# A transformer layer's up-projection: sums moved from GpSimd to VectorE, one block of work spaced wider, one norm written to other tiles

## The chip, the cores and the metric

The kernel runs on one core of a Trainium2 chip. The metric is the device time of one execution in microseconds (us). The kernel before took 2619.06 us (median of three runs, 2615.29 to 2621.99). A profile is one further execution, recorded by the hardware profiler.

The engines are named as the profile names them: PE is TensorE (matrix multiplications), DVE is VectorE, ACT is ScalarE, POOL is GpSimd, SP is SyncE, which here only starts DMA transfers. Each takes its instructions strictly in the order in which they were written for it. An instruction that has to wait holds everything behind it on the same engine.

## The reference

One layer of a diffusion transformer works on 2048 tokens of width 1024, with retention and grouped attention side by side, an output projection, and a feed-forward part of width 4096, all in float32. What matters here is the end of the layer:

```
x  = x + g1 * (concat([ret, att]) @ w_out)
h2 = rmsnorm(x, norm2_g) * (1 + sc2) + sh2
x  = x + g2 * (square(relu(h2 @ w_ff1)) @ w_ff2)
return rmsnorm(x, final_norm_g)
```

`h2 @ w_ff1` is the up-projection, the product with `w_ff2` the down-projection. The part `g2 * (... @ w_ff2)` is computed with g2 multiplied into the columns of `w_ff2`.

## The kernel before

**Numbers.** A float32 matrix is used as two fp16 matrices, a high part (ScalarE rounds) and a low part (VectorE subtracts the high part from the source). Each product of two such matrices takes three multiplications, high by high, high by low and low by high. The two 2x2 block matrices of each product in the feed-forward part are multiplied in the Strassen-Winograd way: seven products P1 to P7 instead of eight, of sums and differences of the blocks. These sums must be made for all three inputs: for `w_ff1` (w1), for h2 (h) and for `w_ff2` (w2).

**Up-projection.** `w_ff1` is cut into 16 blocks of 256 columns, the tokens into two halves. There are 24 items (`ITEMS`): first eight blocks with the first half, then the other eight with both halves, then the first eight with the second half. An item has seven products per half, in the order P1, P2, P6, P5, P7, P3, P4; P6, P7 and P4 accumulate onto P1's PSUM bank, P3 onto P5's. Between these, ScalarE copies the bank (`tap`, L2103) or VectorE adds it to an earlier copy (`add`, L2107), so a product that goes on with a bank waits until the copy or addition before it has read that bank. After an addition ScalarE applies relu (L2108, L2129) and the square (L2112), and SP stores the result (L2135). The first four products are made at the end of the stage before; the other 220 (`JOBS`) are numbered 0 to 219: items with one half are products 0 to 51, items with both halves 52 to 163, the last eight items 164 to 219. One product is twelve multiplications (L2092, L2093, L2094) into 512 columns.

**What each item needs of w1.** `fetch_w1` loads a block two items ahead (L2048, SP, into a ring of four tiles, two per item); `sum_w1` makes four sums of 128x512 float32 (L2060, GpSimd); `hi_w1` (L2065, ScalarE) and `lo_w1` (L2071, VectorE) make the seven high and low parts.

**What runs beside the products.** `h_forms`, four times from product 5 on, ten products apart, forms the second token half of h: four sums (in `seven`, L2154, GpSimd), seven high parts (L2179, ScalarE) and seven low parts (L2184, VectorE and GpSimd in turn). `w2_forms`, sixteen times from product 53 on, forms a block of w2: loads (L2144), a product with g2 of 128x1024 for each of two tiles (`gated`, L2150, GpSimd), the four sums of `seven` (L2154), seven high parts (L2208), seven low parts (L2212), and stores to DRAM (L2216). For products P2 and P4 of w2 (in the last of four rounds only P2) a second level of the scheme is formed: differences of 128x256 (`minus`, L2231, GpSimd), one for each of the first two blocks of a round and three for each of the other two, 56 in all. The tiles of the sums in `seven` come from a ring whose first three buffers have the tag "hu".

**The order** is written out by hand: `on(k, phase, ...)` puts a piece of work at product k, and within a product the phases follow as "begin", "pe", "sum", "hi", "lo", "relu", "out", "square", "late", "dma". So a sum at product k stands on its engine ahead of the low part at product k and of the addition at the end of product k.

**The last row before it.** `output_tile` makes the 16 rows (128 tokens each) of `x + g1 * ...`. The last one, t = 0, ends just as the up-projection begins: the row is stored (`store_x`, L1862), its root mean square is found (L1866, L1566, L1567), the row is multiplied by it in its own tile (`norm`, L1872, GpSimd), and then, in the `rest` steps at product 2 and after, TensorE transposes it (L1877), VectorE scales (L1882), GpSimd shifts (L1887) and SP stores it as h (L1890). The sums of w1 of items 0 and 1 stand on GpSimd around this norm.

**The down-projection** starts after product 219. Its first loads (`fetch_u`, `fetch_w2`) stand on SP from product 210 and 166 on; its sums (L2375, L2391) are on GpSimd.

Of the kernel before, what the change touches and what calls it, by code (L numbers as in the profile page):

```python
# [11 lines left out]
F32 = mybir.dt.float32  # L12
# [5 lines left out]
ALU = mybir.AluOpType  # L18
# [4 lines left out]
P = 128  # L23
# [33 lines left out]
def layer_kernel(ctx: ExitStack, tc: tile.TileContext, a: dict, out: bass.AP):  # L57
    nc = tc.nc
# [5 lines left out]
    ident = const.tile([P, P], F32, name="ident")  # L64
# [215 lines left out]
    with ExitStack() as st, tc.manual_schedule():  # L280
        xp = st.enter_context(tc.tile_pool(name="xp", bufs=4, reuse_waits="tile"))
# [4 lines left out]
        op = st.enter_context(tc.tile_pool(name="op", bufs=2, reuse_waits="tile"))  # L286
# [920 lines left out]
        units, first = [], {}  # L1207
# [10 lines left out]
        for (g, col), w in weights.items():  # L1218
            s = first[g, col]
# [13 lines left out]
        for n, (col, s) in enumerate(((C_RK, 5), (C_AKV, 6), (C_AQ, 12), (C_RQ, 16), (C_RV, 18), (C_RG, 26))):  # L1233
            w = weights[0, col]
            for j in range(w.n):
                at = s + (j if col != C_RV else j > 0)
                to = 1536 + 4 * n if col != C_RG else 1560
# [5 lines left out]
        for n, tile_of in enumerate(GROUPS[1]):  # L1243
            b = first[0, C_RV] + 3 + n + n // 6
            rows, x = Rows([tile_of], 1), {}
# [36 lines left out]
        s = first[1, C_RG]  # L1282
# [210 lines left out]
        for s, (g, col, m) in enumerate(units):  # L1493
            if s < 6:
                continue
            ps = psO.tile([P, 512], F32, name="pso", tag="pso")
# [8 lines left out]
        s = len(units)  # L1505
# [9 lines left out]
    def pool(stack, name, bufs=1, **kw):  # L1515
        return stack.enter_context(tc.tile_pool(name=name, bufs=bufs, reuse_waits="tile", **kw))

    qp = pool(attn, "qp", 2)
    op = pool(attn, "op2", 2)
# [5 lines left out]
    xp = pool(side, "wx", 2, side="right")  # L1525
# [14 lines left out]
    def bank(i, shape=(P, 4, P)):  # L1540
        return psX.tile(list(shape), F32, name=f"bank{i}", tag=f"bank{i}")
# [3 lines left out]
    def on(k, phase, fn, *args):  # L1545
        events.setdefault((k, phase), []).append((fn, args))
# [12 lines left out]
    def settle(what):  # L1559
        while what not in settled:  # L1560
            link()
# [254 lines left out]
    def output_tile(t, k, last):  # L1816
        y = {}
# [51 lines left out]

        def norm():  # L1870
            settle(("f", t))
            nc.gpsimd.tensor_scalar(y["x"], y["x"], y["r"], 1.0, op0=ALU.mult, op1=ALU.mult)  # L1872

        def transpose_x(q):
            y["ps", q] = bank(q if t < 2 else 1)
            for i in range(4):
                nc.tensor.transpose(y["ps", q][:, i], y["x"][:, (4 * q + i) * P : (4 * q + i + 1) * P], ident)  # L1877

        def modulate(q):
            s = slice(4 * q, 4 * q + 4)  # L1880
# [157 lines left out]
    raw1, w1 = {}, {}  # L2038
# [17 lines left out]
    def sum_w1(n, i):  # L2056
        if n < len(ITEMS):
            to, x, y, op = SUMS1[i]
            s = raw1[n, to] = xp.tile([P, 4, P], F32, name="w1s", tag="w1s", bufs=W1S)
            nc.gpsimd.tensor_tensor(s, raw1[n, x], raw1[n, y], op=op)  # L2060

    def hi_w1(n, i):
        if n < len(ITEMS):
# [73 lines left out]
    def seven(b0, source, tiles, gate=False):  # L2137


        x = {}  # L2140

        def fetch(g):
            w = ff["b"].tile([P, 2, 512], F32, "b")
            nc.sync.dma_start(w.rearrange("p a b -> p (a b)"), source(g))  # L2144
            x.update(zip(tiles(g), (w[:, 0], w[:, 1])))
            x["raw", g] = w.rearrange("p a b -> p (a b)")

        def gated(g):
            w = x["raw", g]
            nc.gpsimd.tensor_tensor(w, w, ff["g2"], op=ALU.mult)  # L2150

        def add(to, p, q, at=None):
            x[to] = x[at] if at else ff["bs"].tile([P, 512], F32, "bs")
            nc.gpsimd.tensor_tensor(x[to], x[p], x[q], op=ALU.subtract)  # L2154

        for g in range(2):
            on(b0 - (8 if gate else 5) + g, "dma", fetch, g)
            if gate:
                on(b0 - 2 + g, "sum", gated, g)
        sums = [("t1", "b12", "b11"), ("t2", "b22", "t1"), ("t3", "b22", "b12", "b12"), ("t4", "b21", "t2", "t1")]  # L2160
        for at, s in zip((0, 1, 2, 4), sums):
            on(b0 + at, "sum", add, *s)
        return x
# [28 lines left out]
    def w2_forms(b0, b):  # L2192
        rd, slot = PLACE[b]
        odd, s = slot // 2, slot % 2
        x = seven(
            b0,
            lambda f: a["w_ff2"][0, b * FB + f * P : b * FB + (f + 1) * P, :],
            lambda f: (f"b{f + 1}1", f"b{f + 1}2"),
            True,
        )  # L2200

        def split(at, dst, parts):
            f = {}

            def hi():
                f[0] = ff["w2f"].tile([P, 2, 512], F16, "w2f")
                for hi, _, src in parts(f[0]):
                    nc.scalar.activation(hi, src, AF.Copy)  # L2208

            def lo():  # L2210
                for hi, lo, src in parts(f[0]):
                    nc.vector.tensor_tensor(lo, src, hi, op=ALU.subtract)  # L2212

            def store():
                n = dst.shape[1] if len(dst.shape) == 3 else 1
                nc.sync.dma_start(dst, f[0] if n == 2 else f[0][:, 0])  # L2216

            on(at, "hi", hi)
            on(at + 1, "lo", lo)
            on(at + 3, "dma", store)  # L2220

        def pieces(f, *srcs):
            f = f.rearrange("p q (v n) -> p q v n", v=2)
            if len(srcs) == 1 and srcs[0].shape[-1] == 512:
                return [(f[:, :, 0], f[:, :, 1], srcs[0].rearrange("p (q n) -> p q n", q=2))]
            return [(f[:, q, 0], f[:, q, 1], src) for q, src in enumerate(srcs)]

        L, R = slice(0, 256), slice(256, 512)

        def minus(to, p, q):  # L2230
            nc.gpsimd.tensor_tensor(to(), p(), q(), op=ALU.subtract)  # L2231

        def deep(w, k):
            i = WORDS[w]
            to = wf_d[rd][i]

            def part(c):
                return lambda: x[w][:, c]

            def held(c):  # L2240
                return lambda: kept[i][:, c]

            def hold():
                nc.scalar.activation(kept[i][:, R], x[w][:, R], AF.Copy)

            def first():
                kept[i] = ff["k"].tile([P, 512], F32, name="w2k", tag=f"k{i}")
                minus(held(L), part(R), part(L))

            if not odd:  # L2250
                on(k, "sum", first)
                on(k + 2, "hi", hold)
                split(k + 2, to[:, 0:4:3, s], lambda f: pieces(f, x[w][:, L], kept[i][:, L]))
                return
            on(k, "sum", minus, held(L), part(R), held(L))
            on(k, "sum", minus, held(R), part(R), held(R))
            split(k + 2, to[:, 2:5:2, s], lambda f: pieces(f, kept[i]))
            split(k + 3, to[:, 1:6:4, s], lambda f: pieces(f, x[w]))
            on(k + 4, "sum", minus, held(L), part(L), held(L))
            split(k + 6, to[:, 6, s], lambda f: pieces(f, kept[i][:, L]))  # L2260

        for at, w in enumerate(WORDS):
            if WORDS[w] in DEEP[rd]:
                deep(w, b0 + (0 if w == "b21" else 5))
            else:
                split(
                    b0 + at,
                    wf_d[rd][WORDS[w]][:, slot],
                    lambda f, w=w: [(f[:, 0], f[:, 1], x[w])],
                )  # L2270
# [29 lines left out]
    def up_jobs():  # L2300

        first = {}
        for j, (n, i, hf) in enumerate(JOBS):
            first.setdefault((n, i), j)
            for k in range(4):
                on(j, "pe", up_part, n, i, hf, k)
            on(j, "out", up_out, j, n, i, hf)
        for n in range(len(ITEMS) - 1):
            for i in range(7):
                if (n, i) in first:  # L2310
                    at = first[n, i] + len(ITEMS[n][1]) - 1
                    at += 3 * (n == 1)
                    on(at, "hi", hi_w1, n + 1, i)
                    on(at + 1, "lo", lo_w1, n + 1, i)
            on(first.get((n, 0), 0), "dma", fetch_w1, n + 2)
            if n > 0:
                for i in range(2):
                    on(first[n - 1, 5 + i] + 2 * (n == 1), "sum", sum_w1, n + 1, i)
                    on(first[n, i] + 2 * (n == 1), "sum", sum_w1, n + 1, 2 + i)
        on(11, "dma", lambda: nc.sync.dma_start(ff["g2"], gate_d[1].partition_broadcast(P)))  # L2320
        on(20, "late", lambda: nc.scalar.activation(ff["g2"], ff["g2"], AF.Copy, scale=scw))
        for j in range(4):
            h_forms(5 + 10 * j, j)
        first1 = first[AHEAD, 0]
        for m, b in enumerate(PLACE):
            w2_forms(first1 + 1 + (8 * m if m < 14 else 11 * m - 32), b)
        for i in range(7):
            on(first[NB, 0] + 2 + 6 * i, "dma", fetch_w2, i)

# [319 lines left out]
```

## Time and profile before

| | |
|---|---|
| profiled execution | 2618.28 us |
| its span, first to last instruction | 2616.4 us |
| median of three runs | 2619.06 us |
| granted TensorE clock, mean | 0.996 |
| PE busy | 2577.8 us (99%) |
| DVE busy | 2133.8 us (82%) |
| ACT busy | 1594.3 us (61%) |
| POOL busy | 1842.2 us (70%) |
| up-projection, first to last product | 1446.5 to 2044.3 us |

The 99% of PE is no measure of its speed, since consecutive multiplications overlap and their ends are modelled: a multiplication shows some 379 ns although the next one starts earlier. Where PE really stands shows in the starts. In the rows of a timeline the columns are the start in us, the duration in us, engine, line, operation, output and inputs, count, and in square brackets how long the engine had been idle and what ended that. A row of windows has the window, its width and then the busy time (with the number of instructions) of PE, weight loads, DVE, ACT and POOL, the granted clock, the DMA share and GB/s. A row of groups has the count, then the busy time in us and the mean in ns, then the idle time in front of the group by what ended it. A row of one line's answer has shortest/median/longest in ns.

### The profile page before, as it was taken

The numbers are of one execution on the slowest core, as the hardware profiler recorded it, in microseconds if no ns is written. First come the engines' busy times: TensorE is split into PE (matmuls) and PEld (weight loads), VectorE is DVE, ScalarE is ACT, GpSimd is POOL, SyncE is SP. The second block draws the span as 40 slices with busy tenths as digits, with TensorE's granted clock in tenths as the row PEclk, the third lists the DMA queues.
The fourth block names the chain that finished last, engine by engine and source line by source line (L and its number), as shares of the span: only waits on it lengthen the run. The fifth ranks groups of instructions, "written<-read, shape, count | busy, mean of one in ns | idle before, by whom it ended". The sixth has DMA issues, their size and how long they took to land. (4 is left out here: it accounts for less than half of the span.)

```text
span 2616.4 us, 46757 instructions
## 1 busy us (share of the span) xinstructions
PE 2577.8 (99%) x17121; PEld 1499.6 (57%) x17121; DVE 2133.8 (82%) x3142; ACT 1594.3 (61%) x2779; POOL 1842.2 (70%) x1563
## 2 busy tenths in 40 slices
PE   8999999999999999999999899999999999999998
PEld 5885565546666666666666444444444555555554
DVE  5779789768888888888886576999975688888798
ACT  3865454327778878888787576767666433333344
POOL 3644577637666678788887686999963577777687
PEclk9999999999999999999999999999999999999999
DMA  7877899756121132333323655768686768485643
GB/s 234 284 239 236 269 340 360 230 142 224 46 89 58 58 97 82 98 98 111 96 82 99 234 168 177 249 221 260 217 266 200 258 222 312 174 321 194 217 161 113
DMA packets 343326, 492.94 MB, mean 188 GB/s; under 512 B 90788, under 2 KB 213172, under 8 KB 338616
## 3 DMA queue, kind: packets, MB, share of 16 engines
q1 hardware_dynamic: 343080, 489.95, 56.2%
q8 instruction: 134, 2.20, 0.3%
q14 instruction: 96, 0.79, 0.1%
q10 hardware_dynamic: 16, 0.01, 0.0%
HBM read 327.39 MB, written 161.89 MB: 187 GB/s over the span
## 5 line engine op out<-in xcount | busy, mean ns | idle before, releaser
L200 DVE TENSOR_REDUCE nm<-mp 128x1 f32<-128x512 f32 x558 | 377.9, 684 | 97.8 <-PE mp L187 89.9
L226 ACT ACTIVATE p<-st 128x512 f32<-128x512 f32 x576 | 338.3, 593 | 141.4 <-PE st L221 140.4
L237 POOL TENSOR_TENSOR plo<-p,phi 128x1024 f16<-128x1024 f32 x160 | 349.0, 2187 | 71.0 <-ACT phi L230 69.7
L2092 PE MATMUL pu<-hf,w1f 128*128 128x512 f16 x896 | 341.2, 381 | 11.0 <-DVE r L2107 9.4
L2093 PE MATMUL pu<-hf,w1f 128*128 128x512 f16 x896 | 341.2, 381 | 0.0
L2094 PE MATMUL pu<-hf,w1f 128*128 128x512 f16 x896 | 340.9, 380 | 0.0
L230 ACT ACTIVATE phi<-p 128x1024 f16<-128x1024 f32 x288 | 302.8, 1051 | 0.0
L2412 PE MATMUL pd<-w,uf 128*128 128x512 f16 x672 | 254.7, 379 | 0.6 <-DVE y L2442 0.6
L2414 PE MATMUL pd<-w,uf 128*128 128x512 f16 x672 | 254.7, 379 | 0.0
L2413 PE MATMUL pd<-w,uf 128*128 128x512 f16 x672 | 254.7, 379 | 0.0
L239 DVE TENSOR_TENSOR plo<-p,phi 128x512 f16<-128x512 f32 x256 | 225.5, 883 | 15.3 <-ACT phi L230 13.4
L253 PE MATMUL o<-wv,plo 128*128 128x65 f16 x2304 | 230.0, 193 | 1.6 <-POOL plo L237 1.6
L255 PE MATMUL o<-wv,phi 128*128 128x129 f16 x2176 | 228.3, 220 | 0.0
L220 PE MATMUL st<-qr,ks 128*128 128x512 f16 x576 | 218.1, 379 | 3.6 <-ACT p L226 3.5
L253 PEld LDWEIGHTS <-plo 128*128 128x128 f16 x2304 | 205.1, 98 | 29.0 <-POOL plo L237 3.1
L221 PE MATMUL st<-qr,ks 128*128 128x512 f16 x576 | 218.2, 379 | 0.1
L1203 PE MATMUL pso<-wf,h_l 128*128 128x512 f16 (+1 forms) x576 | 208.1, 361 | 0.0
L1204 PE MATMUL pso<-wf,h_l 128*128 128x512 f16 (+1 forms) x576 | 208.1, 361 | 0.0
L1205 PE MATMUL pso<-wf,h_l 128*128 128x512 f16 (+1 forms) x576 | 208.1, 361 | 0.0
L255 PEld LDWEIGHTS <-phi 128*128 128x128 f16 x2176 | 193.1, 97 | 24.2
L2447 POOL TENSOR_TENSOR y<-y,d 128x512 f32<-128x512 f32 x72 | 107.3, 1493 | 136.0 <-ACT uf L2396 126.1
L187 PE MATMUL mp<-ks,qr 128*128 128x512 f16 x512 | 194.0, 379 | 1.4 <-DVE nm L200 0.6
(413 smaller groups left out, 6768.7 us busy)
## 6 DMA issues: line engine op xcount, KB each, us to landing
wm<-in_w_ff SPq DMA_DIRECT2D x64, 512.0 KB, 6.2
u<-r SPq DMA_DIRECT2D x128, 256.0 KB, 4.6
ur<-u SPq DMA_DIRECT2D x128, 256.0 KB, 4.8
y<-x SPq DMA_DIRECT2D x64, 512.0 KB, 7.8
wf<-w2f SPq DMA_DIRECT2D x126, 256.0 KB, 3.9
w<-wf SPq DMA_DIRECT2D x28, 1024.0 KB, 8.4
w1r<-in_w_ff SPq DMA_DIRECT2D x48, 512.0 KB, 5.3
x<-y SPq DMA_DIRECT2D x48, 512.0 KB, 5.1
```

The source lines that it names most:

```text
L200: nc.vector.tensor_reduce(dst, src, axis=AX.X, op=ALU.max, negate=True)
L226: nc.scalar.activation(self.p[kt // 2][:, kt % 2], self.s.pop(kt), AF.Exp, scale=HD**-0.5)
L230: nc.scalar.activation(hi, self.p[j], AF.Copy)
L237: nc.gpsimd.tensor_tensor(lo, p, hi, op=ALU.subtract)
L253: mm(o[:, : HD + 1], lo[:, i, c], v[:, : HD + 1], start=False, stop=False)
L255: mm(o, hi[:, i, c], v[:, :VW], start=False, stop=last)
L2092: mm(ps, whi, hi, start=k == 0 and at == i, stop=False, **go_on)
L2093: mm(ps, whi, lo, start=False, stop=False, **go_on)
L2094: mm(ps, wlo, hi, start=False, stop=k == 3, **go_on)
L2412: mm(ps, u[:, 0, b], w[:, b, 0], start=b == 0 and at == i, stop=False, **go_on)
L2413: mm(ps, u[:, 0, b], w[:, b, 1], start=False, stop=False, **go_on)
L2414: mm(ps, u[:, 1, b], w[:, b, 0], start=False, stop=b == 3, **go_on)
```

## The change

```diff
         def norm():
             settle(("f", t))
-            nc.gpsimd.tensor_scalar(y["x"], y["x"], y["r"], 1.0, op0=ALU.mult, op1=ALU.mult)
+            y["n"] = [y["x"][:, 512 * q : 512 * q + 512] for q in range(2)]
+            if not last:
+                nc.gpsimd.tensor_scalar(y["x"], y["x"], y["r"], 1.0, op0=ALU.mult, op1=ALU.mult)
+                return
+            for q in range(2):
+                src, y["n"][q] = y["n"][q], xp.tile([P, 512], F32, name="xn", tag="hu", bufs=3)
+                nc.gpsimd.tensor_scalar(y["n"][q], src, y["r"], 1.0, op0=ALU.mult, op1=ALU.mult)
...
-                nc.tensor.transpose(y["ps", q][:, i], y["x"][:, (4 * q + i) * P : (4 * q + i + 1) * P], ident)
+                nc.tensor.transpose(y["ps", q][:, i], y["n"][q][:, i * P : (i + 1) * P], ident)
...
             s = raw1[n, to] = xp.tile([P, 4, P], F32, name="w1s", tag="w1s", bufs=W1S)
-            nc.gpsimd.tensor_tensor(s, raw1[n, x], raw1[n, y], op=op)
+            (nc.vector if n > 1 else nc.gpsimd).tensor_tensor(s, raw1[n, x], raw1[n, y], op=op)
...
             x[to] = x[at] if at else ff["bs"].tile([P, 512], F32, "bs")
-            nc.gpsimd.tensor_tensor(x[to], x[p], x[q], op=ALU.subtract)
+            nc.vector.tensor_tensor(x[to], x[p], x[q], op=ALU.subtract)
...
         def minus(to, p, q):
-            nc.gpsimd.tensor_tensor(to(), p(), q(), op=ALU.subtract)
+            nc.vector.tensor_tensor(to(), p(), q(), op=ALU.subtract)
...
             if n > 0:
-                for i in range(2):
-                    on(first[n - 1, 5 + i] + 2 * (n == 1), "sum", sum_w1, n + 1, i)
-                    on(first[n, i] + 2 * (n == 1), "sum", sum_w1, n + 1, 2 + i)
+                for i in range(4):
+                    on(first[n, i] + 2 * (n == 1), "sum", sum_w1, n + 1, i)
...
         for m, b in enumerate(PLACE):
-            w2_forms(first1 + 1 + (8 * m if m < 14 else 11 * m - 32), b)
+            w2_forms(first1 + 1 + (47 * m // 5 if m < 12 else 11 * m - 18), b)
```

Four things change. The norm of the last row is written in two halves into two tiles of the tag "hu" instead of back into the row's own tile, and the transposes read from there. The sums of w1 from item 2 on, the four sums of `seven` (for h and w2) and the differences of the second level run on VectorE instead of GpSimd. The four sums of w1 for an item stand two products later in items with one half and four later in items with both (they now stand at the steps P1, P2, P6 and P5 of the item before). The blocks of w2 begin 47/5 products apart instead of 8 (the last four 11 apart instead of the last two), so the last one begins at product 200 instead of 186. What is computed stays the same.

## The prediction

> **What bounds the kernel now.** I read the waits of TensorE first, then the timeline around each gap, engine by engine, then the stages and the groups.
>
> ```profile
> PE pu L2092 <- DVE r L2107: 9.4, 2, 7.1
> PE pu L2092 <- ACT r L2103: 1.6, 2, 1.1
> ```
>
> The columns are us in total, times, longest. These two of its waits belong to the up-projection: four times TensorE stood in front of a product. What that cost has to come from start times, since the modelled ends overlap:
>
> ```profile
> 1450.74 0.38 PE L2092 MATMUL pu<-hf,w1f 128*128 128x512 f16 x1
> ...
> 1462.83 0.38 PE L2094 MATMUL pu<-hf,w1f 128*128 128x512 f16 x1
> 1470.33 0.58 PE L2092 MATMUL pu<-hf,w1f 128*128 128x512 f16 x1 [7.12 <-DVE r L2107]
> ...
> 1475.10 1.04 PE L1877 MATMUL bank<-ident,xr 128*128 128x128 f32 x8
> 1946.61 0.38 PE L2094 MATMUL pu<-hf,w1f 128*128 128x512 f16 x1
> 1949.27 0.59 PE L2092 MATMUL pu<-hf,w1f 128*128 128x512 f16 x1 [2.29 <-DVE r L2107]
> ...
> 1952.86 0.38 PE L2092 MATMUL pu<-hf,w1f 128*128 128x512 f16 x1
> 1470.00:1475.00 5.00, 4.67 (x12) 1.69 (x12) 2.20 (x4) 2.47 (x4) 1.26 (x1) 0.52 1.02 373
> ```
>
> From 1450.74 to 1462.83 lie 56 steps, so an undisturbed multiplication costs 12.09/56 = 0.216 us, a product of twelve 2.59. **The first gap**: 1470.33 - 1462.83 - 0.216 = 7.28 us lost, then twelve multiplications in 4.77 us instead of 2.59 (the granted clock was 0.52 in that slice): 2.18 more. **The third**: 1949.27 - 1946.61 - 0.216 = 2.44, then nine in 3.59 instead of 1.94: 1.65. The two waits on ACT r show 1.6 idle; each costs 0.16 more than its idle (7.28 against 7.12), so 1.9. In all 9.46 + 4.09 + 1.9 = 15.45 us; this is the whole prize in this stage, since matrix work is not touched. The Trainium skill's page "TensorE: Matmul & The Clock Gate", section "What's actually happening", lets the clock fall only after an idle window of about 3.4 us; by that the third gap would cost 2.44 alone and the prize be 13.8. Here 2.29 us of idle was enough (0.59 us for the first multiplication after it), so I keep to the rows.
>
> **Why the first gap is there.**
>
> ```profile
> 1449.57 0.32 SPq L1862 DMA_DIRECT2D x<-xr  x1
> 1450.91 0.55 POOL L1567 TENSOR_TENSOR cy_f<-cv_f,half 128x1 f32<-128x1 f32 x1
> 1460.68 1.12 POOL L1872 TENSOR_SCALAR xr<-xr,cy_f 128x1024 f32<-128x1024 f32 x1 [9.22 <-DMA x<-xr]
> 1461.76 1.04 POOL L1887 TENSOR_TENSOR u<-u,s 128x512 f32<-128x512 f32 x1
> ...
> 1467.42 1.71 POOL L2060 TENSOR_TENSOR w1s<-w1r,w1s 128x512 f32<-128x512 f32 x1
> 1453.60 0.69 DVE L1882 TENSOR_TENSOR u<-bank,a 128x512 f32<-128x512 f32 x1
> 1458.07 0.60 ACT L2103 ACTIVATE r<-pu 128x512 f32<-128x512 f32 x1 [0.67 <-PE pu L2094]
> 1466.27 1.95 ACT L2065 ACTIVATE w1f<-w1s,sc 128x512 f16<-128x512 f32 x3 [7.61 <-POOL w1s L2060]
> 1467.02 2.65 DVE L2071 SCALAR_TENSOR_TENSOR w1f<-w1s,sc,w1f 128x512 f16<-128x512 f32 x2 [8.84 <-ACT w1f L2065]
> 1469.60 0.68 DVE L2107 TENSOR_TENSOR r<-pu,r 128x512 f32<-128x512 f32 x1
> ```
>
> The last row's norm overwrites the tile that its own store still reads, so GpSimd stands until 1460.68. Behind it in GpSimd's queue stand four sums of w1; ACT's high parts wait for those, VectorE's low parts for ACT, and behind them in VectorE's queue stands the addition of product P7, which must read its bank before P4 may accumulate into it. That is the 7.12 us.
>
> **The other three gaps** lie late in the up-projection.
>
> ```profile
> 1476.00:1590.00 114.00, 114.00 (x531) 51.69 (x529) 83.20 (x80) 84.58 (x143) 86.11 (x59) 1.00 0.52 160
> 1590.00:1896.00 306.00, 305.54 (x1416) 138.38 (x1415) 287.61 (x246) 210.15 (x390) 269.01 (x170) 1.00 0.71 228
> 1896.00:2044.00 148.00, 144.58 (x663) 65.02 (x661) 87.52 (x100) 96.28 (x166) 76.19 (x54) 0.99 0.75 242
> L2107 DVE TENSOR_TENSOR r<-pu,r x96: 675/679/694, 1454.2 to 2041.8; 128x512 f32<-128x512 f32 x96
> L2212 DVE TENSOR_TENSOR w2f<-bs,w2f x48: 676/1211/2839, 1615.4 to 1976.0; 128x512 f16<-128x512 f32 x42, 128x256 f16<-128x256 f32 x6
> 1945.28 2.79 POOL L2150 TENSOR_TENSOR b<-b,g2b 128x1024 f32<-128x1024 f32 x1
> 1945.79 2.83 DVE L2212 TENSOR_TENSOR w2f<-bs,w2f 128x512 f16<-128x512 f32 x1
> ```
>
> In the stage rows (width, then PE, PEld, DVE, ACT, POOL busy) VectorE is 94% busy in the middle stage and GpSimd 88%. An addition from PSUM keeps to 675 to 694 ns, while one with both inputs in SBUF ranges from 676 to 2839 ns: it stretches when GpSimd works beside it (at 1945.79 it lies over GpSimd's gate product of 2.79 us, and with it the third gap opens). So VectorE is late because GpSimd is busy; its own work is short.
>
> **The change, part by part.**
>
> (1) *The norm.* Two instructions of 512 columns replace one of 1024 (1.12 us); bounds for the pair are 1.12 and 2 x 1.12, I take 1.3. They need not wait for the store: start 1451.46, end about 1452.8. The first shift at L1887 can follow at about 1453.0, the second's input is there at 1454.29 (1453.60 + 0.69). From 1461.76 the two shifts and four sums took 7.37 us (to 1467.42 + 1.71), the second sum 4.5 of it (ACT went on at 1466.27); so they now end near 1460.4, the second sum near 1457.5. ACT is free at 1458.67, gives the high parts by 1460, VectorE the low parts by 1461.5, and the addition of P7 ends near 1462.2; TensorE gets there at 1463.05. Slack 0.8 us, so the whole 9.46 goes (bounds: 9.46, and 6 if each of those VectorE steps meets GpSimd and takes 1.7). The two new tiles take two of three buffers which the h sums use from product 5 on; the transposes release them at product 2, so that costs nothing (a transpose late by three products, 7.8 us, would show). The old tile is freed earlier, which lets a w1 load on SP's queue go that now stands until those transposes.
>
> (2) *The sums on VectorE*: from item 2 on 22 x 4 of w1, 4 x 4 of h, 16 x 4 of w2, making 168 of 512 columns, and 56 of 256 for the deeper level. No row shows such a sum on VectorE; the nearest is L2107 (0.68, f32 out), upper end the 1.48 of what meets GpSimd now, 0.92 for 256 columns:
>
> ```profile
> L2071 DVE SCALAR_TENSOR_TENSOR w1f<-w1r,sc,w1f x72: 736/1150/2897, 1441.6 to 2025.3; 128x512 f16<-128x512 f32 x72
> L2212 DVE TENSOR_TENSOR w2f<-w2k,w2f x42: 410/920/2860, 1615.1 to 1975.6; 128x256 f16<-128x256 f32 x28, 128x512 f16<-128x512 f32 x14
> L2071 DVE SCALAR_TENSOR_TENSOR w1f<-w1s,sc,w1f 128x512 f16<-128x512 f32 x88 | 116.5, 1327 | 9.4 <-ACT w1f L2065 9.4
> L2212 DVE TENSOR_TENSOR w2f<-b,w2f 128x512 f16<-128x512 f32 x64 | 94.1, 1478 | 2.1 <-ACT w2f L2208 2.1
> L2150 POOL TENSOR_TENSOR b<-b,g2b 128x1024 f32<-128x1024 f32 x32 | 86.2, 2702 | 3.7 <-DMA b<-in_w_ff 3.7
> L2060 POOL TENSOR_TENSOR w1s<-w1r 128x512 f32<-128x512 f32 x43 | 66.9, 1555 | 43.8 <-DMA w1r<-in_w_ff 41.2 <-DVE w1f L2071 2.6
> ```
>
> Added: 168 x 0.68 + 56 x 0.41 = 137 us, at most 168 x 1.48 + 56 x 0.92 = 300. I take the low end, since what stretched them is leaving. Taken away: GpSimd keeps the gate products (86 us) and twelve low parts of h (about 18, at the 1.5 of its sums), a quarter of its 431 us (86.11 + 269.01 + 76.19). The stretch on VectorE is some 325 two-SBUF instructions (7 low parts of w1 for each of 22 items, 64 + 48 + 42 of w2, 16 of h) at about 0.6 us over their floor (1327 and 1478 ns against 736 and 676) = 195 us; three quarters of it is 146. VectorE: 458 (83.20 + 287.61 + 87.52) + 137 - 146 = 449 of 568 us. Its total hardly moves, but no single instruction is held 2.8 us except beside one of 32 gate products, and GpSimd, freed, runs those as soon as their loads land, ahead of the block's other work.
>
> (3) *The spacing*: 47/5 instead of 8 products per block takes 15% of w2's load per time out of the middle stage, and puts four blocks instead of two into the last one. A block costs VectorE (154 x 0.68 + 64 x 0.68 + 56 x 0.41)/16 = 10.7 us at most, so two more and 28 sums of w1 (19 us) fit into the 60 us that it idles there (148 - 87.52). The last block moves from product 186 to 200 of 220, and its stores stand on SP just ahead of the down-projection's first loads:
>
> ```profile
> 2023.55 1.27 POOL L2375 TENSOR_TENSOR us<-ur 128x512 f32<-128x512 f32 x1 [22.03 <-DMA ur<-u]
> ```
>
> Those land 18 us before the last addition of the up-projection (2041.8, in the row of L2107), so stores that hold SP for some us cost nothing; delayed by more than that, each us counts.
>
> (4) *New waits on VectorE.* A sum now waits there for its w1 load; behind it stand the additions, and for them TensorE. GpSimd waited 41.2 us on these loads because it ran ahead of TensorE. VectorE is held in step by the additions, and the sums stand two to four products later than they did, seven products (18 us) after the load is issued:
>
> ```profile
> 1895.01 5.22 SPq L2048 DMA_DIRECT2D w1r<-in_w_ff  x2
> 1905.44 1.28 POOL L2060 TENSOR_TENSOR w1s<-w1r 128x512 f32<-128x512 f32 x1 [6.87 <-DMA w1r<-in_w_ff]
> ```
>
> The load of item 18 lands 10.4 us after SP took it up. The third gap stands ahead of product 184, the last of item 18; the new place of that item's first sum is product 171, so near 1946.8 - 13 x 2.59 = 1913, 8 us after the landing. Cost nothing; without that cover each us late beyond one product (2.59) is a us of TensorE.
>
> **Sum**, against the profiled execution's 2618.28 us (span 2616.4): -9.46 and -6.0, plus 1.2 for what stays beside the gate products (half of the 2.44, estimated) = 2604.0. The median of the runs is 0.8 above the profiled execution: 2604.8.
>
> **Rivals.** *A: the late gaps stay.* Against VectorE the gate products still stand, 2.7 us each. A two-SBUF instruction that meets one waits for it, and in the last stage the addition of P7 has only one product before P4 needs its bank. Then only the first gap goes: 2618.3 - 9.5 = 2608.8, median 2609.6. The Trainium skill's "SBUF — State Buffer", section "Who interferes with whom", says that the shared port pair is an exclusive lock held for a whole instruction; by that rule each gate product can still hold VectorE, and the trace agrees (2.83 beside 2.79).
> *B: the first gap is mostly refilled*, as P7's addition has 0.8 us of slack only, or P4's operand lands late behind the same loads as the store. If 6 of the 9.46 stay, 2618.3 - 3.5 - 4.8 = 2610.0, median 2610.8, at the edge of "same".
> *C, slower: VectorE becomes the bound.* If the stretch does not fall, because the gate products and low parts left on GpSimd meet as many instructions, VectorE needs 458 + 137 = 595 of 568 us: 27 over, so 2618.3 - 9.5 + 27 = 2635.8. It decides from a fall of the stretch by less than about 27 of its 195 us. With GpSimd down to a quarter that is unlikely.
> *D: the change does nothing for the norm*, since its new tiles wait for their buffers: 2618.3 - 4.8 = 2613.5.
>
> **Chances.** Forecast 0.58, A 0.22, B 0.10, C 0.05, D 0.05. A measurement of this kernel can tell about 0.3%, 7.9 us, from no change: below 2611.2 is faster. Forecast and A are (0.80); B and D are "same", with some of B's spread either way: faster 0.80, same 0.14, slower 0.06. Range: the least is all 15.45 plus spread of the runs, 2600; the top, to hold 8 in 10, reaches through A to 2612.
>
> **What would show it.** Norm at 1451 to 1453 with no DMA wait; no start gap at 1463; L2212 and L2071 near 0.7 us; VectorE below 90% in the middle stage; GpSimd below 150 us. Wrong if TensorE's wait on DVE r stays above 5 us, or a VectorE wait on w1r or b loads appears with TensorE idle behind it.

## The result, and the profile after

| | before | changed |
|---|---|---|
| median (range) of five runs each, us | 2619.06 (2615.29 to 2621.99) | 2605.84 (2603.75 to 2608.21) |
| profiled execution, us | 2618.28 | 2603.75 |
| up-projection, start of first to start of last product, us | 1446.54 to 2043.94 | 1446.82 to 2029.55 |
| lost in it in front of and between multiplications, us | 15.66 | 0.99 |
| from there to the end of the span, us | 572.5 | 572.5 |

The ratio is 0.9947, with an interval of 0.9936 to 0.9958: 13.2 us faster, against 14.3 predicted; by the 0.3% that the prediction set as its bound, faster. "Lost" is summed over the starts of the up-projection's multiplications in a profiled execution: each distance to the next start less the undisturbed 0.216 us, where it is over 0.02 us. The stage became 597.40 - 582.73 = 14.67 us shorter, and that is the whole difference; what stands before and after it took the same time.

TensorE's waits in the changed kernel (us in total, times, longest) hold one row for the bank of a product where there were two with 11.0 us together:

```profile
PE pu L2098 <- DVE r L2113: 0.6, 2, 0.4
```

The timeline around the place of the first gap, engine by engine:

```profile
1463.11 0.38 PE L2100 MATMUL pu<-hf,w1f 128*128 128x512 f16 x1
1463.76 0.38 PE L2098 MATMUL pu<-hf,w1f 128*128 128x512 f16 x1 [0.27 <-DVE r L2113]
...
1449.85 0.32 SPq L1862 DMA_DIRECT2D x<-xr  x1
...
1451.19 0.55 POOL L1567 TENSOR_TENSOR cy_f<-cv_f,half 128x1 f32<-128x1 f32 x1
1451.85 1.84 POOL L1878 TENSOR_SCALAR xn<-xr,cy_f 128x512 f32<-128x512 f32 x2
1453.82 1.47 POOL L1893 TENSOR_TENSOR u<-u,s 128x512 f32<-128x512 f32 x1
...
1460.84 1.71 POOL L2066 TENSOR_TENSOR w1s<-w1r,w1s 128x512 f32<-128x512 f32 x1
...
1459.23 1.33 ACT L2071 ACTIVATE w1f<-w1s,sc 128x512 f16<-128x512 f32 x2 [0.29 <-POOL w1s L2066]
...
1459.99 3.11 DVE L2077 SCALAR_TENSOR_TENSOR w1f<-w1s,sc,w1f 128x512 f16<-128x512 f32 x2 [0.24 <-ACT w1f L2071]
1463.02 0.68 DVE L2113 TENSOR_TENSOR r<-pu,r 128x512 f32<-128x512 f32 x1
```

The store is issued at 1449.85 as before, but the norm now starts at 1451.85, right behind the factor that it needs, instead of 9 us later behind the store. What followed it moved up by as much; of the gap of 7.28 us and its slow multiplications 0.43 us is left, because the two low parts at 1459.99 took 3.11 us together beside GpSimd's last two sums and the addition behind them ends at 1463.70, just after TensorE is there.

The windows of the up-projection: 568 us up to its end in both kernels, then the middle stage of the changed kernel (width, then busy time of PE, PEld, DVE, ACT and POOL, the clock, DMA share, GB/s):

```profile
1476.00:2044.00 568.00, 564.12 (x2606) 255.09 (x2604) 458.33 (x425) 391.01 (x697) 431.31 (x281) 1.00 0.69 218
```

```profile
1462.00:2030.00 568.00, 567.37 (x2633) 257.55 (x2632) 448.98 (x655) 397.18 (x704) 114.76 (x59) 1.00 0.69 222
1590.00:1880.00 290.00, 290.00 (x1345) 131.52 (x1344) 230.93 (x344) 195.91 (x358) 63.09 (x24) 1.00 0.66 213
```

VectorE got 224 more instructions on the whole page and 9 us less to do here; in the middle stage it is 80% busy (230.93 of 290) instead of 94%. GpSimd went from 431 to 115 us. One group of the 568 us of before, then the groups of the changed kernel (count, busy us and mean ns, idle before) show why:

```profile
L2212 DVE TENSOR_TENSOR w2f<-b,w2f 128x512 f16<-128x512 f32 x56 | 87.6, 1573 | 2.1 <-ACT w2f L2208 2.1
```

```profile
L2077 DVE SCALAR_TENSOR_TENSOR w1f<-w1s,sc,w1f 128x512 f16<-128x512 f32 x91 | 75.6, 835 | 7.1 <-ACT w1f L2071 7.1
L2218 DVE TENSOR_TENSOR w2f<-b,w2f 128x512 f16<-128x512 f32 x56 | 48.9, 879 | 1.5 <-ACT w2f L2214 1.5
L2066 DVE TENSOR_TENSOR w1s<-w1r 128x512 f32<-128x512 f32 x44 | 36.8, 835 | 0.0
L2066 DVE TENSOR_TENSOR w1s<-w1s,w1r 128x512 f32<-128x512 f32 x22 | 15.0, 684 | 0.0
...
L2237 DVE TENSOR_TENSOR w2k<-b,w2k 128x256 f32<-128x256 f32 x24 | 9.4, 419 | 0.0
...
L2156 POOL TENSOR_TENSOR b<-b,g2b 128x1024 f32<-128x1024 f32 x32 | 83.4, 2618 | 322.7 <-DMA b<-in_w_ff 281.1 <-DVE w2f L2218 19.8 <-DVE r L2113 14.5
```

The low parts of w1 that took 1327 ns take 835, and those of w2 go from 1573 to 879. (The 1478 ns in the prediction is a mean over 64 low parts of w2, eight of which have only 256 columns.) A sum costs 684 ns where nothing meets it, and 419 ns with 256 columns, as the two prices were taken from L2107 (0.68) and the 410 ns row. Here GpSimd runs almost nothing but the 32 gate products.

### The profile page after: what moved, and what is told of

The parts are those of the page before. It is cut to its first block, busy times and chain, and to the rows that moved or that the text cites. A ratio compares the mean times of both kernels' runs of the same rounds, so it can differ in the third digit from the quotient of the medians.

```text
span 2602.0 us, 46647 instructions
## 1 busy us (share of the span) xinstructions
PE 2574.0 (99%) x17121; PEld 1498.6 (58%) x17121; DVE 2122.0 (82%) x3366; ACT 1597.8 (61%) x2779; POOL 1525.9 (59%) x1340
## 4 chain that ended last, share of the span: by engine, by line
PE 85%; DMA 5%; DVE 4%; ACT 2%; POOL 2%; issue 2%; SPq 0%; ACTq 0%; DVEq 0%; POOLq 0%
PE pu L2098 7%; PE pu L2099 7%; PE pu L2100 7%; PE pd L2417 5%; PE pd L2419 5%; PE pd L2418 5%; PE st L220 4%; PE o L255 4%; PE st L221 4%; PE pso L1204 4%; PE pso L1203 4%; PE pso L1205 4%; PE mp L187 4%; PE o L253 2%; PE bank L1847 2%; PE bank L1846 2%
## 5 line engine op out<-in xcount | busy, mean ns | idle before, releaser
L2098 PE MATMUL pu<-hf,w1f 128*128 128x512 f16 x896 | 339.6, 379 | 0.6 <-DVE r L2113 0.6
L2100 PE MATMUL pu<-hf,w1f 128*128 128x512 f16 x896 | 339.6, 379 | 0.0
L2156 POOL TENSOR_TENSOR b<-b,g2b 128x1024 f32<-128x1024 f32 x32 | 83.4, 2618 | 322.7 <-DMA b<-in_w_ff 281.1
```

Source lines behind the costliest of these rows:

```text
L2098: mm(ps, whi, hi, start=k == 0 and at == i, stop=False, **go_on)
L2100: mm(ps, wlo, hi, start=False, stop=k == 3, **go_on)
```

## The experiments

In each profiled execution, one for each kernel, the lost time was summed as above. It is sharper here than the medians, since the stages ahead of the up-projection differ by some us from run to run (its first product starts between 1446.5 and 1453.8 in these profiles). Unless said otherwise the computation is unchanged. Line numbers behind L1870 shift by up to eight between the kernels: the addition is L2107, L2113 or L2115, and the first multiplication of a product L2092, L2098 or L2100.

| | median (range), us | ratio to before (interval) | lost, us | first gap | VectorE, GpSimd busy of 568 us |
|---|---|---|---|---|---|
| before | 2619.06 | | 15.66 | 9.46 | 458, 431 |
| changed | 2605.84 | 0.9947 (0.9936 to 0.9958) | 0.99 | 0.43 | 449, 115 |
| norm alone | 2610.99 (2606.21 to 2613.78) | 0.9968 (0.9958 to 0.9978) | 7.20 | 0.44 | 458, 431 |
| changed, old norm | 2613.61 (2612.91 to 2617.11) | 0.9983 (0.9975 to 0.9992) | 10.13 | 9.6 | 444, 118 |
| changed, old spacing | 2606.24 (2605.18 to 2607.81) | 0.9953 (0.9940 to 0.9967) | 1.05 | 0.43 | 449, 121 |
| norm and spacing, no sums moved | 2611.16 (2608.46 to 2613.76) | 0.9971 (0.9959 to 0.9982) | 4.83 | 0.43 | 439, 432 |
| changed, gate products on VectorE | 2606.33 (2603.89 to 2610.27) | 0.9954 (0.9941 to 0.9966) | 0.48 | 0.44 | 434, 32 |
| changed, w1 sums twice | 2617.25 (2611.68 to 2618.51) | 0.9991 (0.9982 to 1.0000) | 11.59 | 0.43 | 502, 113 |
| changed, old places of w1 sums | 2606.55 (2602.99 to 2606.99) | 0.9951 (0.9937 to 0.9964) | 0.99 | 0.45 | 445, 117 |
| changed, h and w2 sums back | 2611.41 (2607.55 to 2618.16) | 0.9973 (0.9962 to 0.9984) | 6.83 | 0.43 | 457, 305 |
| changed, w1 sums back | 2609.59 (2606.14 to 2611.40) | 0.9956 (0.9942 to 0.9970) | 5.22 | 0.43 | 451, 245 |
| w1 sums twice, gate products on VectorE | 2608.24 (2606.68 to 2610.15) | 0.9955 (0.9943 to 0.9968) | 4.23 | 0.43 | 487, 31 |

### The norm, alone and taken out

The kernel before with the new norm only:

```diff
-            nc.gpsimd.tensor_scalar(y["x"], y["x"], y["r"], 1.0, op0=ALU.mult, op1=ALU.mult)
...
+            for q in range(2):
+                src, y["n"][q] = y["n"][q], xp.tile([P, 512], F32, name="xn", tag="hu", bufs=3)
+                nc.gpsimd.tensor_scalar(y["n"][q], src, y["r"], 1.0, op0=ALU.mult, op1=ALU.mult)
```

> The kernel before with the new norm alone (sums stay on GpSimd, blocks of w2 8 products apart). My theory: the first gap (9.5 us) goes and the three late gaps (6.0 us) stay, as nothing changed on GpSimd and VectorE there: about 2609.6 us, and TensorE still waits 3 to 4 us on the banks late in the up-projection. Rival, that the sums on VectorE carry the gain: 2617 to 2619 us.

And the changed kernel with the old norm (the same lines the other way round):

> The changed kernel with the norm written back into the row's own tile, waiting for its store again. My theory: the first gap comes back whole (7.3 us of standing, 2.2 us of slow clock), the late ones stay away: 2605.8 + 9.0 = about 2614.8 us. Rival, that GpSimd freed of the later sums has no queue left to delay, so the wait of the norm costs nothing: 2606 us.

TensorE's waits on the banks, first in the kernel with the norm alone, then in the changed kernel with the old norm:

```profile
PE pu L2098 <- DVE r L2113: 2.6, 2, 2.3
PE pu L2098 <- ACT r L2109: 2.1, 2, 1.1
```

```profile
PE pu L2092 <- DVE r L2107: 7.3, 2, 6.9
```

The norm alone brings the first gap down to 0.44 us and leaves the three late ones. It is worth 8.0 us by the medians, 15.66 - 7.20 = 8.5 by the lost time. Taking it out of the changed kernel brings back the wait of 6.9 us and the slow multiplications behind it, and no late gap but one of 0.52 us, as in the changed kernel: 10.13 - 0.99 = 9.1 us lost, 7.8 by the medians. The gain of the norm doesn't need the moved sums, nor theirs the norm, and the norm's is the larger one.

### The spacing, alone and taken out

```diff
-            w2_forms(first1 + 1 + (47 * m // 5 if m < 12 else 11 * m - 18), b)
+            w2_forms(first1 + 1 + (8 * m if m < 14 else 11 * m - 32), b)
```

> The changed kernel with the blocks of w2 8 products apart again. My theory: with sums on VectorE its instructions are short and it has a fifth of its time over, so the spacing is worth next to nothing: 2605 to 2607 us, VectorE busier in the middle stage (some 90%) and no gap above 1 us. Rival, that the spacing is what closed the late gaps: three to six us of gaps come back, 2609 to 2612 us.

The other way round: the kernel before with the new norm and the new spacing, all sums on GpSimd at their old places.

> The kernel before with the new norm and the new spacing, all sums still on GpSimd. My theory: the stretch beside GpSimd stays (low parts of w2 at a mean of 1.2 us or more) and so do gaps of 2 to 6 us, some of them in the last stage, which has two blocks more: 2606.5 to 2610 us. Rival, that spacing alone relieves VectorE: no gap above 1 us and 2605.8 us, the moved sums worth nothing.

Waits and middle stage of the changed kernel with the old spacing:

```profile
PE pu L2098 <- DVE r L2113: 0.7, 2, 0.4
```

```profile
1590.00:1896.00 306.00, 306.00 (x1420) 138.65 (x1418) 266.07 (x397) 214.74 (x398) 73.89 (x26) 1.00 0.73 236
```

The same two views of the kernel with norm and spacing but no sums moved:

```profile
PE pu L2098 <- DVE r L2113: 3.6, 3, 2.3
PE pu L2098 <- ACT r L2109: 0.6, 1, 0.6
```

```profile
1590.00:1896.00 306.00, 306.00 (x1419) 138.67 (x1418) 237.18 (x232) 208.15 (x378) 240.31 (x156) 1.00 0.67 216
```

The spacing does what it says (VectorE 87% busy with the old one, 266.07 of 306, against 80%) and is worth nothing that these runs can tell: 1.05 us lost instead of 0.99, a median 0.4 us higher with overlapping ranges. Without the moved sums it takes VectorE from 94% to 78% of the middle stage, and the late gaps stay: 0.43 is the first gap, 4.4 are late (its median lies 1 us above what was expected). So how full VectorE is over a stage is not what makes these gaps; two of the three of before lie after 1896, where it was 59% busy (87.52 of 148).

### Where the stretch comes from: no GpSimd beside VectorE

```diff
-            nc.gpsimd.tensor_tensor(w, w, ff["g2"], op=ALU.mult)
+            nc.vector.tensor_tensor(w, w, ff["g2"], op=ALU.mult)
```

> The changed kernel with the 32 gate products of w2 (128x1024) on VectorE too, so that GpSimd is nearly empty in the up-projection. My theory, that two-SBUF instructions stretch only beside GpSimd's: the low parts keep to 0.75 us at the mean too, VectorE's busy time stays near 450 us (32 x 1.2 more, the rest of the stretch less), no gap late: 2605 to 2606 us, the time of the changed kernel. Rival, that they stretch for another reason (their own order, the loads): means stay at 0.8 to 0.95 us. Second rival: instructions of 1.2 us on VectorE delay the additions and gaps of 1 to 3 us open.

The whole stretch and two of its groups with the gate products on VectorE:

```profile
1468.50:2036.50 568.00, 567.72 (x2636) 257.82 (x2634) 433.86 (x687) 398.46 (x705) 32.09 (x27) 1.00 0.69 223
```

```profile
L2156 DVE TENSOR_TENSOR b<-b,g2b 128x1024 f32<-128x1024 f32 x32 | 38.9, 1217 | 0.0
L2218 DVE TENSOR_TENSOR w2f<-b,w2f 128x512 f16<-128x512 f32 x56 | 37.9, 683 | 0.1
```

VectorE gets another 38.9 us of work and is busy 434 us instead of 449. The low part of w2 is at its floor of 683 ns; those of w1 come to 783 ns, since twelve low parts of h still run on GpSimd early in the stretch (from 1535 us on, behind most of these, means of 758 and 753 ns). So GpSimd's work is shown as the cause of the stretch: 15 us less with 39 us more to do, so by this sum 54 us of the 449 were still waiting, beside 32 gate products of 2618 ns. No late gap is left. The time does not follow (2606.33, beside 2605.84 of the changed kernel), because only 0.5 us was there to be had. The Trainium skill's page "SBUF — State Buffer", section "Who interferes with whom", says that an instruction of VectorE with two inputs in SBUF contends with one of GpSimd that reads SBUF; this trace agrees, with 879 ns beside the gate products and 683 without.

### Only half of the sums moved

The changed kernel with the sums for h and w2 and the differences back on GpSimd:

```diff
-            nc.vector.tensor_tensor(x[to], x[p], x[q], op=ALU.subtract)
+            nc.gpsimd.tensor_tensor(x[to], x[p], x[q], op=ALU.subtract)
...
-            nc.vector.tensor_tensor(to(), p(), q(), op=ALU.subtract)
+            nc.gpsimd.tensor_tensor(to(), p(), q(), op=ALU.subtract)
```

> The changed kernel with the sums of h and w2 and the second-level differences back on GpSimd; the sums of w1 stay on VectorE. My theory, that lateness follows GpSimd's busy time (some 300 us instead of 125): low parts of w2 at a mean of 1.0 to 1.3 us, gaps of 1 to 3 us in all, 2607 to 2609 us. Rival, that the sums of w1 alone closed the late gaps: 2605.8 us. Second rival, that sums split over two engines cost more than either: above 2611 us.

And with the sums of w1 back there, at their old places (the edit of the places is the one shown in the next section):

```diff
-            (nc.vector if n > 1 else nc.gpsimd).tensor_tensor(s, raw1[n, x], raw1[n, y], op=op)
+            nc.gpsimd.tensor_tensor(s, raw1[n, x], raw1[n, y], op=op)
```

> The changed kernel with the sums of w1 back on GpSimd at their places of before; the sums of h and w2 and the differences stay on VectorE. GpSimd is then busy some 260 us of the up-projection. My theory, lateness follows the time in which GpSimd works beside VectorE: low parts of w1 at a mean of 1.0 to 1.15 us, gaps of 2 to 6 us, 2607 to 2611 us, as with the sums of w1 alone moved. Rival, that the chain of a w2 block over three engines made the late gaps, and that it is enough to take GpSimd out of it: below 1.5 us of gaps, 2605.5 to 2606.5 us.

The waits of the first (only w1's sums moved), its low parts over the same 568 us, and the waits of the second (only those of h and w2 moved):

```profile
PE pu L2098 <- DVE r L2113: 4.5, 4, 2.4
```

```profile
L2077 DVE SCALAR_TENSOR_TENSOR w1f<-w1s,sc,w1f 128x512 f16<-128x512 f32 x88 | 103.2, 1180 | 5.9 <-ACT w1f L2071 5.9
```

```profile
PE pu L2098 <- DVE r L2113: 3.8, 4, 1.6
PE pu L2098 <- ACT r L2109: 0.5, 1, 0.5
```

Neither half closes the late gaps in these profiles. Counted without the slow multiplications that follow some of them, these gaps sum to 0.62 + 1.29 + 2.44 = 4.35 us before, 4.9 with the norm alone, 4.4 with the spacing too, 4.7 with w1's sums moved, 4.7 with those of h and w2 moved, and 0.5 when both are. GpSimd's 431 us fell to 305 and 245 in the two halves, without effect on these gaps; at 115 nearly all was gone. With w1's sums alone, time and gaps lie above the theory (2607 to 2609 us, 1 to 3 us of gaps). The median of 2611.41 is the number of the second rival, but a split that costs more than no move isn't shown: 6.83 us are lost, 7.20 with the norm alone. With those of h and w2 alone, both lie within what the theory expected; its five runs spread from 2606.14 to 2611.40, and the profiled one is among the longest, so a shorter one may have had smaller gaps. The stretch itself does follow GpSimd's time (low parts of w1 at 1327 ns before, 1180 and 1096 in the two halves, 835 in the changed kernel); the gaps don't.

The traces show where the step comes from: not GpSimd's total counts, but what it does in the few products ahead of the addition that TensorE waits for. These are the 10.4 us (four products) ahead of the addition at the largest late gap, before, in the two halves, and in the changed kernel:

```profile
1938.14:1948.54 10.40, 8.85 (x41) 3.89 (x40) 10.40 (x5) 4.09 (x8) 10.32 (x6) 1.00 1.03 363
1967.19:1977.59 10.40, 8.70 (x41) 3.83 (x40) 10.40 (x8) 4.06 (x7) 10.08 (x6) 1.00 0.99 336
1969.24:1979.64 10.40, 9.55 (x45) 4.20 (x43) 10.40 (x6) 4.79 (x9) 9.70 (x6) 1.00 1.06 351
1961.66:1972.06 10.40, 10.40 (x50) 4.69 (x49) 9.88 (x10) 6.01 (x11) 4.77 (x2) 1.00 1.04 370
```

In all four, two gate products lie there. In each half GpSimd still has sums or differences to make around them and is busy 10.08 and 9.70 of the 10.4 us, as before (10.32); VectorE has 8 and 6 instructions in that time, where it has 10 when GpSimd runs the two gate products alone (4.77).

### The places of the sums of w1

```diff
-                for i in range(4):
-                    on(first[n, i] + 2 * (n == 1), "sum", sum_w1, n + 1, i)
+                for i in range(2):
+                    on(first[n - 1, 5 + i] + 2 * (n == 1), "sum", sum_w1, n + 1, i)
+                    on(first[n, i] + 2 * (n == 1), "sum", sum_w1, n + 1, 2 + i)
```

> The changed kernel with the sums of w1 at their places of before (two products earlier in items of one half, four in the others), but on VectorE. My theory: loads land 10 us after their issue and the earliest old place is five products (13 us) after it, so VectorE waits on few of them, 0 to 2 us of gaps: 2606 to 2608 us. Rival, that the later places are what keeps VectorE from standing on loads: it waits several us for w1r in most of the last items and TensorE behind it, 2610 to 2618 us.

TensorE's waits with the sums on VectorE at the old places:

```profile
PE pu L2098 <- ACT r L2109: 0.3, 1, 0.3
PE pu L2098 <- DVE r L2113: 0.3, 1, 0.3
```

0.99 us are lost, as in the changed kernel, and in neither does VectorE wait for a load of w1. The later place cost nothing and was not needed.

### How much room VectorE has

Each sum of w1 from item 2 on is made twice on VectorE, the second time with the same result:

```diff
             (nc.vector if n > 1 else nc.gpsimd).tensor_tensor(s, raw1[n, x], raw1[n, y], op=op)
+            if n > 1:
+                nc.vector.tensor_tensor(s, raw1[n, x], raw1[n, y], op=op)
```

> The changed kernel with each sum of w1 from item 2 on made twice on VectorE, the same result written again: 88 x 0.6 = 53 us more on VectorE. My theory, that VectorE has some 119 us over and only its lateness at single points matters: gaps of 0 to 3 us in all, 2606 to 2609 us. Rival, that VectorE is near its bound already: most of the 53 us shows, above 2620 us.

The same, with the gate products on VectorE as well:

> The changed kernel with the sums of w1 twice on VectorE and the gate products on VectorE too: about 60 us more work than with the gate products on VectorE alone, and GpSimd nearly empty. Theory A, that the gaps of the run with doubled sums need a gate product beside VectorE (2.7 us at once on top of a fuller queue): at most 3 us of gaps, 2606 to 2609 us. Theory B, that the fuller queue alone makes VectorE late where items of one half leave one product of slack: 7 us or more of gaps, above 2612 us.

With the sums twice: waits, the stretch, and the timeline ahead of one of the late gaps (TensorE stood from 1921.45 to 1923.45):

```profile
PE pu L2100 <- DVE r L2115: 7.6, 5, 2.3
PE pu L2100 <- ACT r L2111: 0.9, 2, 0.4
```

```profile
1473.50:2041.50 568.00, 559.73 (x2582) 252.85 (x2581) 501.51 (x735) 390.57 (x694) 113.04 (x56) 1.00 0.67 215
```

```profile
1915.01 2.73 POOL L2158 TENSOR_TENSOR b<-b,g2b 128x1024 f32<-128x1024 f32 x1 [3.83 <-DVE r L2115]
...
1915.55 2.73 DVE L2068 TENSOR_TENSOR w1s<-w1r 128x512 f32<-128x512 f32 x1
...
1922.71 0.68 DVE L2115 TENSOR_TENSOR r<-pu,r 128x512 f32<-128x512 f32 x1
```

With the gate products on VectorE too:

```profile
PE pu L2100 <- DVE r L2115: 2.4, 3, 1.3
PE pu L2100 <- ACT r L2111: 0.7, 2, 0.5
```

The 88 sums are 60 us of work (0.68 each), which a stretch with 119 us of idle time on VectorE should have swallowed; they cost 10.6 us of lost time (11.4 by the medians), where 0 to 3 us were expected. VectorE stood idle for 66 of the 568 us and was still late: P4 needs P7's addition one product later, in items with one half, so the room that counts is that of one product. A sum held for 2.73 us by a gate product uses up more than the 2.59 of it; three gaps of 1.78, 2.30 and 2.44 us lie in the last stage, the third with slow multiplications behind it. With the gate products gone 0.97 is left there. Another 2.8 us lie between 1483 and 1525, where the forms of h run; they are there in both kernels (1.46 us the largest in each), so they need no gate product. That the fuller queue alone makes them isn't shown: GpSimd still makes its low parts of h there (in the second kernel two instructions of VectorE, at 1512.06 and 1517.59, took 1.65 and 1.53 us beside them), and VectorE waits some 2.9 us for a load of h ahead of the later three of these gaps. The 4.23 us lost in the second kernel lie between what either theory expected (its median of 2608.24 lies in the range of A): most of the damage is a gate product falling onto a full queue, but not all of it.

## Why the prediction was right, and where it was not

**The sum** -9.46 - 6.0 + 1.2 = -14.3 us came out as -14.5 between the profiled executions (-14.4 of span). The 1.2 for what stays was 0.52 late and 0.43 at the first gap; that these come near 1.2 together is luck, since the forecast left nothing at the first gap.

**(1) The norm.** Right, shown by both experiments on it. The pair took 1.84 us, not 1.3, and P7's addition ended at 1463.70, not 1462.2: the two low parts ahead of it met GpSimd's sums and took 3.11 us together, near the 1.7 us each of the bound. The 0.8 us of slack was therefore used up, and rival B's mechanism is there, at 0.43 us instead of 6. No wait of the new tiles on their buffers (rival D), and no transposes late.

**(2) The sums on VectorE.** The cause was right: with GpSimd's work gone from beside them, VectorE's instructions shrink. The forecast of 449 us is the 449 of the window, but that close a match is partly luck, as the terms were less exact. By their groups the sums took 155 us (66.8 + 66.4 + 22.3 over the rows of L2066, L2160 and L2237), not 137, since some met a gate product (means of 835 and 684 ns in the same line). The low parts fell by 150 us, from 418 to 268 by their groups, where 146 were forecast. Added alone that would leave VectorE 6 us busier; but the groups add up durations that overlap at their ends (494 us of them make 449 of busy time, 485 made 458 before), and that hid the difference. The sign of low parts near 0.7 us wasn't reached (means of 786 to 950 ns at 512 columns), since the gate products still hold some of them. Rival A fell: what the gate products still cost is 0.5 us. The prediction had one cause for the late gaps, VectorE being late because GpSimd is busy, and that holds product by product; how it depends on the amount of GpSimd's work the prediction didn't ask, and the runs with half of the sums show that it isn't in proportion.

**(3) The spacing.** The load moved as forecast, without a price and without a gain. The argument that its load must leave the middle stage was not needed.

**(4) The new waits.** VectorE waits for no load of w1, and that the later place gives the cover wasn't needed either. One new wait did appear, 1.4 us for a load of h ahead of a sum of `seven` (1500.65, L2160), with no gap of TensorE behind it, so the prediction's sign of being wrong was not met.

**The step that fails is rival C's deciding point.** It said that VectorE becomes the bound when its work exceeds the 568 us of the stretch, from a fall of the stretch by less than 27 us. At 502 us, with the sums of w1 made twice, it had already cost 11 us, so the chance of 0.05 rested on more room than there was. Nor is there another total that decides: the kernels with half of the sums lose 4.7 us late at 457 and 450 us, the changed kernel 0.5 at 449. The same reading misled the part on the spacing, which reckoned with whole stages.

**The third gap's 1.65 us for the slow clock**, kept because a row showed it, is not a fixed price of such an idle time, as the last section shows. The forecast had 4.09 for that gap; a wait of the same length elsewhere (2.31 us, with norm and spacing) cost its standing alone, 2.47 us.

## What to carry to other kernels

When VectorE's instructions with two inputs in SBUF range from 0.7 to 2.8 us, look at what GpSimd does beside them: moving GpSimd's work of the same kind onto the "full" engine can leave it no fuller, but here only the whole move closed the late gaps, and half of it left them as long as they were. An overwrite in place had to wait 9.2 us here for a store that still read the tile, and so had everything queued behind it. The idle share of a stage is not the room for more work where a single instruction must come within one product; measure that room by adding work on purpose.

## What the runs showed of the hardware

The granted clock after an idle time was less regular than the profile of before suggests. Starts of TensorE behind two waits of the same length, in the kernel with the norm alone and in the one with norm and spacing:

```profile
1941.26 0.38 PE L2098 MATMUL pu<-hf,w1f 128*128 128x512 f16 x1 [2.29 <-DVE r L2113]
...
1942.21 0.63 PE L2099 MATMUL pu<-hf,w1f 128*128 128x512 f16 x1
...
1945.54 0.38 PE L2098 MATMUL pu<-hf,w1f 128*128 128x512 f16 x1
```

```profile
1980.95 0.38 PE L2098 MATMUL pu<-hf,w1f 128*128 128x512 f16 x1 [2.31 <-DVE r L2113]
1981.16 0.38 PE L2099 MATMUL pu<-hf,w1f 128*128 128x512 f16 x1
```

After 2.29 us of idle the first four starts are 0.22 us apart, then some 3.4 us run at half speed (0.43 us a step), then full speed again. After 2.31 us in the other kernel nothing slows. In the profile of before the slow stretch began at once. Its window and the one ahead of it, then two windows of the kernel with norm and spacing, around its wait:

```profile
1945.81:1949.22 3.41, 1.18 (x6) 0.42 (x5) 3.41 (x4) 0.00 (x0) 3.41 (x2) 1.00 0.82 282
1949.22:1952.64 3.42, 3.37 (x9) 1.17 (x9) 3.42 (x4) 2.47 (x4) 3.42 (x4) 0.50 0.87 206
```

```profile
1976.02:1979.43 3.41, 2.62 (x13) 1.07 (x11) 3.41 (x2) 0.00 (x0) 3.41 (x2) 1.00 1.06 323
1979.43:1982.84 3.41, 1.89 (x9) 0.88 (x9) 3.41 (x5) 1.91 (x4) 3.41 (x3) 1.00 0.93 314
```

In the up-projection it came after idle times of 2.28 to 2.43 us in four of five cases, at once or up to 1 us after the restart, and lasted about 3.4 us in each, 1.6 to 1.8 us lost; after 2.14 and less it never came there, after 7 us each time. The Trainium skill's page "TensorE: Matmul & The Clock Gate", section "What's actually happening", says that activity is judged over a window of 3413 ns that runs freely. The length of the slow stretch and its shifting start agree with that; that a whole idle window is needed does not, since 2.3 us were enough.

What decides is how much of the idle time falls into one window, and the traces show it. In each of the twelve profiles the recorded changes of the granted clock lie whole multiples of 3413 ns apart (to within some ns), so the windows can be laid out in time, and TensorE's idle time, as the profile has it, be summed in each. In the up-projection every window at full clock with 2.24 us or more of idle time was followed by one at half clock (six, 2.24 to 3.41 us), and none with 1.58 us or less was. The 2.29 us of before lay nearly whole in one window (3.41 - 1.18 = 2.23 in its row); the 2.31 us of the other kernel were split over two, 0.79 and 1.52. Over the whole executions, 9082 windows at full clock, the border lies near half a window: each of the 20 with 1.83 us or more was followed by half clock, none of those with 1.62 us or less, and one of the three between, at 1.65 to 1.69 us.
